# A one-layer hybrid encoder on one core: memory's loads and transposes moved ahead, a row factor put into the rotary tables

## The chip, the cores and the metric

One NeuronCore of a Trainium2 chip runs the whole layer as one program. The metric is device microseconds of an execution, the median of several runs. All data are float32. Each large product is made of three TensorE products of float32r parts (high times high, high times low, low times high), so a weight or an activation is first split into a rounded part and a rest.

## The reference

One layer, with 512 positions of 1024 features, and 256 memory rows of 1024 features:

```python
h = rmsnorm(x, pre_mix_g)
aq, ak, av, hq, hf_fwd, hf_bwd, hi, hg = split_columns(h @ w_in, IN_SPLITS)
aq = rmsnorm(aq per head, q_norm_g); ak = rmsnorm(ak per head, k_norm_g)
att = axial_gqa_attention(apply_rope(aq, cos, sin), apply_rope(ak, cos, sin), av)
rec = hgrn2_group(hq, hf_fwd, hf_bwd, hi, hg, lb, out_g)
x = x + rmsnorm(concatenate([att, rec]) @ w_out, post_mix_g)
h, m = rmsnorm(x, pre_x_g), rmsnorm(mem, mem_norm_g)
x = x + rmsnorm(memory_cross_attention(h, m, w_xq, w_xkv, w_xo), post_x_g)
h = rmsnorm(x, pre_ffn_g)
x = x + rmsnorm(conv_ffn(h, w_up, conv_w, conv_b, w_down), post_ffn_g)
```

Attention has 8 query heads of 64 on 2 key heads; the recurrent group (HGRN2) has 4 heads of 128 and runs in both directions.

## The kernel before

Weights arrive as 132 units of 128x1024, in the order of use. A unit is loaded on SP's queue (L117) and split: units 7 to 41 by a cast on ScalarE (`wh`, L127), a negation (`wl`, units 7 to 27 on ScalarE, L129; 28 to 41 on GpSimd, L131) and a DMA on GpSimd's queue that adds the weight to `wl` in flight (L132); the others by a cast (L104) and a subtraction on VectorE (L105). Three units are prepared ahead of the one in use. TensorE multiplies them at L150, L151 and L152.

Row 1/rms(x) is never multiplied into x: the projections use x times the gain, and each output row is scaled by `r` afterwards.

The mixing stage weaves two streams of program text. One, `mix_projections`, holds the projections: the output gate (`put_sg`), the three projections of heads 1, 2 and 3 (`hgrn_in`), the queries, and keys and values (`put_kv`). The other, `cores`, holds the recurrences of heads 0, 1 and 2 (`hgrn_core`). A recurrence goes level by level: a copy on ScalarE (L514), eight small products (L517, PSUM bank tag `ps_c`), multiplications and a predicated copy on VectorE (L543, L549); then L524, L529, L534, L555 to L557, the squares of its output (L561), the row factor on GpSimd (L168, L169) and a transpose (L571). A scheduling layer then fixes each engine's order of instructions by its own estimates, and each engine runs its list strictly in order; a wait holds all that is behind it on that engine. Loads that ScalarE or GpSimd issue stand in the same list as its arithmetic.

Memory's part of this stage: `mem_norm` asks for the norm's weight (L163) and memory's two blocks of 128 rows (L660) on GpSimd's queue, squares them on ScalarE (L203) and scales them on VectorE (L185). `mem_turn` transposes them on TensorE (L194) through the two PSUM banks `ps_b`, with a split to high and low parts after each (L104, L105). Their projections to keys begin when the mixing projections are over.

Queries and keys go through `norm_rope`: squares (L594), a sum per head (L596), the power -1/2 on GpSimd (L168, L169), a multiplication of that factor by `r` on GpSimd (L598), and on VectorE two products with the rotary tables (L603, L606), their sum (L607) and the product with the head's factor (L608). The tables, cosine and sine times the gains of the norms, are made once by `rope_tables` from a load on GpSimd's queue (L581). For keys a cast (L618) and a subtraction (L619) follow, and `turn_k` transposes the result into `kT` (L626, copied out by L627) through the same banks `ps_b` as the memory keys (`put_kx`) use at that time.

All pools are shared: 16 buffers `big`, and PSUM banks in pairs with the tags b, s, o and c.

Of the kernel before, what the change touches and what calls it, by code (L numbers as in the profile page):

```python
# [14 lines left out]
ALU = mybir.AluOpType  # L15
# [3 lines left out]
P = 128  # L19
D = 1024  # L20
T = 512
NB = T // P
KC = D // P
M = 256
MB = M // P
# [4 lines left out]
AHEAD = 3  # L30
HOLD_BLOCK = 4
TURN_STEP, MEM_TURN, UP_TURN = 0, (0, 4), (0, 2)
NEG_SCALAR = frozenset(range(7, 28))
NEG_POOL = frozenset(range(28, 42))
CORE_SHARE, ATT_LEAD = 53.0, 4.0
KEY_TURNS = {1: (0, 1), 2: (2, 3)}
WARM, SPREAD_STEP = 4, 2
# [37 lines left out]
def layer(tc, io, out):  # L75
    nc = tc.nc
# [14 lines left out]
    def bank(tag):  # L91
        return ps.tile([P, 512], F32, name="ps_" + tag, tag=tag)

    def big(shape, dt=F32):
        return b8.tile(shape, dt, name="big", tag="big")
# [7 lines left out]
    def split(hi, lo, src, eng=None):  # L103
        nc.scalar.copy(hi, src)  # L104
        (eng or nc.vector).tensor_sub(lo, src, hi.bitcast(F32))  # L105
# [15 lines left out]
    def issue():  # L121
# [3 lines left out]
        wl = wp.tile([P, 1024], F32R, name="wl", tag="wl")  # L125
        if i in NEG_SCALAR or i in NEG_POOL:
            nc.scalar.copy(wh, raw)  # L127
            if i in NEG_SCALAR:
                nc.scalar.mul(wl, wh.bitcast(F32), -1.0)  # L129
# [24 lines left out]
    def blk(b):  # L154
        return slice(b * P, (b + 1) * P)

    def rows_bc(src, n):
        return src[None, :].to_broadcast([P, n])

    def gains(*names, eng=None):  # L160
        g = big([P, 2, D])
        for i, name in enumerate(names):
            (eng or nc.gpsimd).dma_start(g[:, i, :], rows_bc(io[name], D))  # L163
        return [g[:, i, :] for i in range(len(names))]
# [7 lines left out]
    def half(c):  # L172
        return slice(c * 512, c * 512 + 512)
# [10 lines left out]
    def scale_rows(xb, r, g, h, c):  # L184
        nc.vector.scalar_tensor_tensor(out=h[:, half(c)], in0=xb[:, half(c)], scalar=r, in1=g[:, half(c)],  # L185
                                       op0=ALU.mult, op1=ALU.mult)

    def turn_in(h, act, b, tags, before=None):
        for c in range(2):
            if before:  # L190
                before(c)
            o = bank(tags[c]).rearrange("p (k n) -> p k n", k=4)
            for k in range(4):
                nc.tensor.transpose(o[:, k, :], h[:, blk(c * 4 + k)], ident)  # L194
            hi, lo = act.hi, act.lo
            if len(hi) == 2:
                split(hi[c][:, :, blk(b)], lo[c][:, :, blk(b)], o)
            else:
                split(hi[0][:, c * 4:c * 4 + 4, blk(b)], lo[0][:, c * 4:c * 4 + 4, blk(b)], o)
# [62 lines left out]
    def proj_tm(act, tags, use, n=512):  # L262
        o = [bank(t) for t in tags]
        nk = 1024 // n
        for j in range(8 // nk):
            w = unit(nk)
            for b in range(len(tags)):
                for k in range(nk):
                    kc = nk * j + k
                    mm3(o[b][:, :n], act.get(kc, blk(b)), (w[0][:, k, :], w[1][:, k, :]), kc == 0, kc == 7)  # L270
                if kc == 7:
                    use(b, o[b])
                yield 3 * nk * MM * n / 512
# [121 lines left out]
    r = rstd_of(rx[:, :NB], NB, D, rx[:, NB:])  # L395
# [48 lines left out]
    sg_box, heads, qkv, rec_done = [], {}, {}, [0]  # L444
# [20 lines left out]
    def hgrn_in(h, between=()):  # L465
        qk = big([P, 2, 2, T])
        tt = big([P, 2048])
        q = tmp2(tag="tq")

        def put_q(z):  # L470
            nc.scalar.activation(q, z, ACT.Sigmoid)
            nc.vector.tensor_mul(q, z, q)

        def put_f(d):
            def put(z):
                f = tt[:, d * T:(d + 1) * T]
                k = qk[:, 1, d, :]
                nc.scalar.activation(f, z, ACT.Sigmoid)
                nc.scalar.activation(k, z, ACT.Sigmoid, scale=-1.0)
                nc.scalar.activation(f, f, ACT.Identity, scale=oml[:, d, h:h + 1], bias=lb[:, d, h:h + 1])  # L480
                nc.vector.scalar_tensor_tensor(out=qk[:, 0, 1 - d, :], in0=f, scalar=oml[:, d, h:h + 1], in1=q,
                                               op0=ALU.mult, op1=ALU.mult)
            return put

        for put in (put_q, put_f(0), put_f(1)):
            yield from proj_fm(hT, T, "b", scaled(put))
            for job in between[:3]:
                job()
            between = between[3:]
        heads[h] = (q, qk, tt)  # L490
# [85 lines left out]
        yield 0.5  # L576

    def rope_tables():
        both = big([P, 6, NB, 64])
        rope, cs = both[:, 0:4], both[:, 4:6]  # L580
        nc.gpsimd.dma_start(cs, io["rope"])  # L581
        nc.vector.tensor_scalar(qkg[:, 0, :], qkg[:, 0, :], 0.125, None, op0=ALU.mult)
        for i in range(2):
            nc.vector.tensor_mul(rope[:, 2 * i], cs[:, 0], qkg[:, None, i, :].to_broadcast([P, NB, 64]))
            gs = pat(qkg, i * 64 + 1, [[0, NB], [2, 32], [-1, 2]])
            nc.vector.tensor_tensor(out=rope[:, 2 * i + 1].rearrange("p b (i two) -> p b i two", two=2),
                                    in0=cs[:, 1].rearrange("p b (i two) -> p b i two", two=2), in1=gs, op=ALU.mult)
        return rope

    def norm_rope(z, nh, which, b):  # L590
        n = nh * 64
        rope = qkv["rope"]
        u = tmp2()
        nc.scalar.activation(u[:, :n], z, ACT.Square, scale=r[:, b:b + 1])  # L594
        ss = small()
        nc.vector.tensor_reduce(ss[:, :nh], u[:, :n].rearrange("p (h d) -> p h d", h=nh), axis=AX.X, op=ALU.add)  # L596
        rz = rstd_of(ss[:, :nh], nh, 64)
        nc.gpsimd.tensor_scalar(rz[:, :nh], rz[:, :nh], r[:, b:b + 1], 0.0, op0=ALU.mult, op1=ALU.add)  # L598
        xn = tmp2()
        x3 = xn[:, :n].rearrange("p (h d) -> p h d", h=nh)  # L600
        st = rope[:, 2 * which + 1, b, :]
        ss4 = st.rearrange("p (i two) -> p i two", two=2)[:, None].to_broadcast([P, nh, 32, 2])
        nc.vector.tensor_tensor(out=u[:, :n].rearrange("p (h i two) -> p h i two", h=nh, two=2),  # L603
                                in0=pat(z, 1, [[64, nh], [2, 32], [-1, 2]]), in1=ss4, op=ALU.mult)
        ct = rope[:, 2 * which, b, :][:, None, :].to_broadcast([P, nh, 64])
        nc.vector.tensor_tensor(out=x3, in0=z.rearrange("p (h d) -> p h d", h=nh), in1=ct, op=ALU.mult)  # L606
        nc.vector.tensor_add(xn[:, :n], xn[:, :n], u[:, :n])  # L607
        nc.vector.tensor_tensor(out=x3, in0=x3, in1=rz[:, :nh, None].to_broadcast([P, nh, 64]), op=ALU.mult)  # L608
        return x3
# [12 lines left out]
    def turn_k(b):  # L622
# [3 lines left out]
            nc.tensor.transpose(o[:, i, :].bitcast(F32R), kd4[:, i, :], ident_r)  # L626
        nc.scalar.copy(qkv["kT"][:, :, blk(b)], o)  # L627

    def open_qkv():
        qkv["rope"] = rope_tables()  # L630
        qkv["kT"] = big([P, 4, T], F32R)
        qkv["vv"] = const.tile([P, NB, 2, 2, 64], F32R, name="vv")
        qkv["qT"] = [big([P, 4, T], F32R) for _ in range(2)]
# [18 lines left out]

    kv = {}

    def mem_norm():
        g_mem, = gains("mem_norm_g")
        kv["rows"] = big([P, MB, D])
        for b in range(MB):
            m = kv["rows"][:, b, :]
            nc.gpsimd.dma_start(m, io["mem"][blk(b), :])  # L660
            r = row_rstd(m, tmp4([P, D]))
            for c in range(2):
                scale_rows(m, r, g_mem, m, c)

    def mem_turn():
        kv["m"] = Act([big([P, 8, M], F32R)], [big([P, 8, M], F32R)])
        for b in range(MB):
            turn_in(kv["rows"][:, b, :], kv["m"], b, "bb")

    def mix_projections():  # L670
        yield from proj_tm(hT, tm_tags, put_sg)
        yield from hgrn_in(1)
        mem_norm()
        yield from hgrn_in(2)
        open_qkv()
        zs, roped = {}, {}
        yield from proj_tm(hT, tm_tags, zs.__setitem__)

        def rope_job(b):
            return lambda: roped.__setitem__(b, rope_q(b, zs[b]))  # L680

        def turn_job(b):
            return lambda: turn_q(b, roped[b])

        jobs = [rope_job(0), rope_job(1)]
        for b in range(NB):
            jobs.append(turn_job(b))
            if b + 2 < NB:
                jobs.append(rope_job(b + 2))
        mem_turn()  # L690
        yield from hgrn_in(3, jobs)
        yield from proj_tm(hT, tm_tags, put_kv, 256)

# [356 lines left out]
```

## Time and profile before

| what | value |
|---|---|
| median of 3 runs (lowest, highest) | 852.19 us (851.39, 852.71) |
| the profiled execution's own time | 850.9 us |
| its span, first to last instruction | 849.0 us |
| mean granted TensorE clock | 0.993 |
| TensorE busy | 831.3 us, 98% of the span |
| VectorE busy | 490.7 us, 58% |
| ScalarE busy | 426.4 us, 50% |
| GpSimd busy | 102.7 us, 12% |

In the rows of a timeline the first number is the start in microseconds from the beginning of the span and the second the duration; the bracket at the end gives how long the engine stood idle before the row and what ended that. A matmul's duration includes its way through the array, so consecutive rows overlap: the pace is the distance between starts. A row of several equal instructions carries their count.

### The profile page before, as it was taken

How to read it: one execution, taken by the hardware profiler on the slowest of the kernel's cores; microseconds unless marked ns; L12 is line 12 of the kernel's file. 1: busy time of each engine (PE TensorE's matmuls, PEld its weight loads, DVE VectorE, ACT ScalarE, POOL GpSimd, SP SyncE). 2: the span in 40 equal slices, each digit the busy share in tenths (PEclk: the TensorE clock that was granted, in tenths of full speed). 3: DMA queues.
4: the chain of work that ended last, by engine and by line, in shares of the span. 5: the costliest groups of instructions: out<-in, count | busy, mean ns of one | idle time of the engine just before them, and what ended most of it. 6: DMA issues, size and time to landing. Idle time of an engine off the chain costs nothing.

```text
span 849.0 us, 11082 instructions
## 1 busy us (share of the span) xinstructions
PE 831.3 (98%) x4304; PEld 705.0 (83%) x4304; DVE 490.7 (58%) x759; ACT 426.4 (50%) x736; POOL 102.7 (12%) x163
## 2 busy tenths in 40 slices
PE   9999999999899999999999999999999999999996
PEld 7888777889799888888888998888888888888885
DVE  5364487479786875854443865555555557722224
ACT  6675656467688874644543643333333335511121
POOL 0111211057223201300001300000000000000001
PEclk9999999999899999999999999999999999999999
DMA  8686854556667633252312243223332332222212
GB/s 313 189 200 136 223 126 96 107 142 146 157 143 167 138 117 132 75 174 75 101 48 75 76 135 97 95 94 100 100 100 99 100 100 81 100 95 96 100 49 100
DMA packets 29796, 101.81 MB, mean 120 GB/s; under 512 B 3952, under 2 KB 4464, under 8 KB 29744
## 3 DMA queue, kind: packets, MB, share of 16 engines
q1 hardware_dynamic: 22752, 77.38, 27.0%
q0 software_dynamic: 6272, 22.81, 14.4%
q10 hardware_dynamic: 720, 0.92, 0.3%
q8 instruction: 34, 0.56, 0.3%
q14 instruction: 18, 0.15, 0.1%
HBM read 99.00 MB, written 2.10 MB: 119 GB/s over the span
## 4 chain that ended last, share of the span: by engine, by line
PE 92%; ACT 2%; POOL 2%; DMA 1%; DVE 1%; issue 1%; POOLq 0%; DVEq 0%; ACTq 0%
PE ps_b L150 9%; PE ps_b L151 9%; PE ps_b L152 9%; PE ps_s L152 6%; PE ps_s L151 6%; PE ps_s L150 6%; PE ps_o L150 6%; PE ps_o L152 6%; PE ps_o L151 6%; PE ps_c L151 4%; PE ps_c L150 4%; PE ps_c L152 4%; PE ps_c L517 3%; PE ps_o L754 2%; PE ps_s L732 2%; PE ps_o L742 2%
## 5 line engine op out<-in xcount | busy, mean ns | idle before, releaser
L105 DVE TENSOR_TENSOR wl<-raw,wh 128x1024 fp32r<-128x1024 f32 x93 | 113.8, 1223 | 199.6 <-ACT wh L104 199.5
L104 ACT CAST wh<-raw 128x1024 fp32r<-128x1024 f32 x93 | 98.0, 1053 | 205.2 <-PE ps_o L152 71.4
L150 PE MATMUL ps_b<-big,wh 128*128 128x512 f32 (+1 forms) x320 | 119.5, 373 | 0.0
L152 PE MATMUL ps_b<-big,wl 128*128 128x512 f32 (+1 forms) x320 | 118.0, 369 | 0.0
L151 PE MATMUL ps_b<-big,wh 128*128 128x512 f32 (+1 forms) x320 | 117.9, 368 | 0.0
L152 PEld LDWEIGHTS ps_b<-big,wl 128*128 128x128 f32 x320 | 61.5, 192 | 9.4
L151 PEld LDWEIGHTS ps_b<-big,wh 128*128 128x128 f32 x320 | 61.6, 193 | 9.3
L150 PEld LDWEIGHTS ps_b<-big,wh 128*128 128x128 f32 x320 | 61.5, 192 | 9.2
L178 POOL TENSOR_SCALAR small<-small 128x1 f32<-128x1 f32 x40 | 13.9, 348 | 439.1 <-ACT tmp L209 420.2
L543 DVE TENSOR_TENSOR big<-big 128x512 f32<-128x512 f32 x64 | 47.3, 747 | 17.6 <-PE ps_c L517 12.7
L150 PE MATMUL ps_s<-wh,big 128*128 128x512 f32 (+1 forms) x140 | 53.7, 383 | 0.0
L151 PE MATMUL ps_s<-wl,big 128*128 128x512 f32 (+1 forms) x140 | 53.2, 380 | 0.0
L152 PE MATMUL ps_s<-wh,big 128*128 128x512 f32 (+1 forms) x140 | 53.2, 380 | 0.0
L127 ACT CAST wh<-raw 128x1024 fp32r<-128x1024 f32 x35 | 36.6, 1048 | 31.1 <-PE ps_b L151 17.5
L150 PE MATMUL ps_o<-wh,big 128*128 128x512 f32 (+1 forms) x124 | 47.8, 386 | 0.0
L151 PE MATMUL ps_o<-wl,big 128*128 128x512 f32 (+1 forms) x124 | 47.0, 379 | 0.0
L152 PE MATMUL ps_o<-wh,big 128*128 128x512 f32 (+1 forms) x124 | 46.8, 378 | 0.0
L132 POOL DMA_DIRECT2D wl<-in_w_dram x35 | 31.0, 886 | 115.8 <-ACT wl L129 104.2
L105 DVE TENSOR_TENSOR big<-ps_o,big 128x512 fp32r<-128x512 f32 x52 | 35.7, 687 | 13.4 <-ACT big L104 13.2
L104 ACT CAST big<-ps_o 128x512 fp32r<-128x512 f32 x52 | 30.5, 586 | 19.4 <-PE ps_o L857 7.5
L517 PE MATMUL ps_c<-big,tmp 128*128 128x128 f32 x224 | 33.4, 291 | 4.1 <-ACT tmp L514 3.2
L517 PEld LDWEIGHTS ps_c<-big,tmp 128*128 128x128 f32 x224 | 30.3, 194 | 8.4 <-ACT tmp L514 6.4
(246 smaller groups left out, 1961.0 us busy)
## 6 DMA issues: line engine op xcount, KB each, us to landing
raw<-in_w_dram SPq DMA_DIRECT2D x131, 512.0 KB, 3.3
wl<-in_w_dram POOLq DMA_DIRECT2D x35, 512.0 KB, 5.5
big<-in_x_dram SPq DMA_DIRECT2D x8, 512.0 KB, 6.2
big<-in_xt_dram SPq DMA_DIRECT2D x3, 512.0 KB, 8.5
big<-in_mem_dram POOLq DMA_DIRECT2D x2, 512.0 KB, 8.2
out_dram<-big SPq DMA_DIRECT2D x4, 256.0 KB, 2.0
out_dram<-big ACTq DMA_DIRECT2D x3, 256.0 KB, 2.0
big<-in_xt_dram SPq DMA_DIRECT2D x2, 256.0 KB, 3.5
```

The costliest lines, as they stand in the source:

```text
L104: nc.scalar.copy(hi, src)
L105: (eng or nc.vector).tensor_sub(lo, src, hi.bitcast(F32))
L127: nc.scalar.copy(wh, raw)
L132: nc.gpsimd.dma_start(wl, io["w"][i], accum_op=ALU.add)
L150: nc.tensor.matmul(o, a[0], b[0], start=start, stop=False)
L151: nc.tensor.matmul(o, a[0], b[1], start=False, stop=False)
L152: last_mm[0] = nc.tensor.matmul(o, a[1], b[0], start=False, stop=stop).ins
L517: nc.tensor.matmul(o[:, b, :], kc[:, blk(b)], pat(qk, b * P, [[2 * m, P // (2 * m)], [T + m, 2], [1, m]]), start=True, stop=True)
L543: nc.vector.tensor_tensor(out=c, in0=c, in1=pat(tt, toff + off, [[2, npair], [gap, 2], [0, m]]), op=ALU.mult)
L732: nc.tensor.matmul(s, qT[h // 4][:, h % 4, blk(qb)], kT[:, 2 * (h // 4) + c, :], start=c == 0, stop=c == 1)
L742: nc.tensor.transpose(o[:, c, :], e[:, 0, blk(c)], ident)
L754: nc.tensor.matmul(o, vv[:, c, h // 4].rearrange("p a d -> p (a d)"), pt[:, j, c, :], start=c + j == 0, stop=c == 3 and j == 1)
```

## The change

Four things are changed. The names in the diff are those of the section on the kernel; line numbers after the first part shift by up to nine in the new file.

- Memory's norm weight, its two row blocks (`mem_load`) and the rotary tables (`load_tables`) are asked for on ScalarE's queue, at the start of `mix_projections`. Before, they were asked for on GpSimd's queue where they are used.
- `r` is multiplied into cosine and sine, once per block of 128 positions, by four small ScalarE instructions (L581 of the new file); the multiplication on GpSimd in each `norm_rope` (L598) is gone, eight instructions in all.
- `mem_turn` stands between the projections of head 2 and the queries, no longer behind the queries, and its transposes use the banks `ps_s` and `ps_o`, which the projection of the queries takes right behind it.
- Units 28, 29 and 30 are negated on ScalarE (L129) and no longer on GpSimd (L131).

```diff
-NEG_SCALAR = frozenset(range(7, 28))
-NEG_POOL = frozenset(range(28, 42))
+NEG_SCALAR = frozenset(range(7, 31))
+NEG_POOL = frozenset(range(31, 42))
...
     def rope_tables():
-        both = big([P, 6, NB, 64])
-        rope, cs = both[:, 0:4], both[:, 4:6]
-        nc.gpsimd.dma_start(cs, io["rope"])
+        rope, cs = qkv["tables"][:, 0:4], qkv["tables"][:, 4:6]
+        for b in range(NB):
+            nc.scalar.mul(cs[:, :, b, :], cs[:, :, b, :], r[:, b:b + 1])
...
         rz = rstd_of(ss[:, :nh], nh, 64)
-        nc.gpsimd.tensor_scalar(rz[:, :nh], rz[:, :nh], r[:, b:b + 1], 0.0, op0=ALU.mult, op1=ALU.add)
...
+    def load_tables():
+        qkv["tables"] = big([P, 6, NB, 64])
+        nc.scalar.dma_start(qkv["tables"][:, 4:6], io["rope"])
...
-    def mem_norm():
-        g_mem, = gains("mem_norm_g")
+    def mem_load():
+        kv["g"], = gains("mem_norm_g", eng=nc.scalar)
         kv["rows"] = big([P, MB, D])
         for b in range(MB):
+            nc.scalar.dma_start(kv["rows"][:, b, :], io["mem"][blk(b), :])
+
+    def mem_norm():
+        for b in range(MB):
             m = kv["rows"][:, b, :]
-            nc.gpsimd.dma_start(m, io["mem"][blk(b), :])
...
-            turn_in(kv["rows"][:, b, :], kv["m"], b, "bb")
+            turn_in(kv["rows"][:, b, :], kv["m"], b, "so")
...
     def mix_projections():
+        mem_load()
+        load_tables()
         yield from proj_tm(hT, tm_tags, put_sg)
         yield from hgrn_in(1)
         mem_norm()
         yield from hgrn_in(2)
+        mem_turn()
         open_qkv()
...
-        mem_turn()
         yield from hgrn_in(3, jobs)
```

ScalarE's list in the first recurrence (head 0), before; `wh` and `wl` are parts of weight units, L478 to L480 the gates of head 0, L502, L508 and L514 belong to the recurrence:

```order
L127 CAST wh<-raw 128x1024 x2
L129 ACTIVATE wl<-wh 128x1024
L478 ACTIVATE big<-tmp_442 128x512
L479 ACTIVATE big<-tmp_442 128x512
L480 ACTIVATE big<-big,lb,oml 128x512
L129 ACTIVATE wl<-wh 128x1024
L502 ACTIVATE tmp_466<-big,oml 128x512
L514 COPY tmp_481<-big 128x512
L127 CAST wh<-raw 128x1024
```

And the same place now:

```order
L127 CAST wh<-raw 128x1024
L163 DMA big<-in_mem_norm_g_dram 128x1024
L129 ACTIVATE wl<-wh 128x1024
L478 ACTIVATE big<-tmp_442 128x512
L479 ACTIVATE big<-tmp_442 128x512
L480 ACTIVATE big<-big,lb,oml 128x512
L662 DMA big<-in_mem_dram 128x1024 x2
L630 DMA big<-in_rope_dram 128x512
L127 CAST wh<-raw 128x1024
L502 ACTIVATE tmp_473<-big,oml 128x512
L129 ACTIVATE wl<-wh 128x1024
L514 COPY tmp_488<-big 128x512
```

Four DMA issues have come in, and one cast and one negation of weights have changed places with the recurrence's first steps. In TensorE's list the first products of this recurrence (L507) now stand behind 20 more products of the gate's projection than before.

GpSimd's list where keys are normalised (`small` holds the heads' factors), before:

```order
L169 TENSOR_TENSOR small<-small,nhalf 128x2
L598 TENSOR_SCALAR small<-small,rx 128x2
L131 TENSOR_SCALAR wl<-wh 128x1024
L132 DMA wl<-in_w_dram 128x1024
L168 TENSOR_SCALAR small<-small 128x2
```

And now:

```order
L169 TENSOR_TENSOR small<-small,nhalf 128x2
L168 TENSOR_SCALAR small<-small 128x2
L169 TENSOR_TENSOR small<-small,nhalf 128x2
L132 DMA wl<-in_w_dram 128x1024
L168 TENSOR_SCALAR small<-small 128x2
```

The multiplication by `r` and the negation have gone from between the powers; the first L131 now stands behind the last key's power.

TensorE's list at the end of head 1's recurrence (L571 is its output's transpose, `ps_s` and `ps_o` the projection of the queries), before:

```order
L152 MATMUL ps_s<-wh,big 128x512
L150 MATMUL ps_o<-wh,big 128x512
L151 MATMUL ps_o<-wl,big 128x512
L571 MATMUL ps_c<-ident,tmp_1063 128x128
L152 MATMUL ps_o<-wh,big 128x512
L571 MATMUL ps_c<-ident,tmp_1063 128x128 x2
```

And now (L194 are memory's transposes):

```order
L150 MATMUL ps_b<-big,wh 128x512
L151 MATMUL ps_b<-big,wh 128x512
L152 MATMUL ps_b<-big,wl 128x512
L194 MATMUL ps_s<-ident,big 128x128 x4
L194 MATMUL ps_o<-ident,big 128x128 x4
L194 MATMUL ps_s<-ident,big 128x128 x4
L194 MATMUL ps_o<-ident,big 128x128 x4
L571 MATMUL ps_c<-ident,tmp_1065 128x128 x3
L150 MATMUL ps_s<-wh,big 128x512
```

Memory's 16 transposes have come here from behind the queries; they now stand ahead of L571, where before only products of the projections did.

More of the change, by code (lines that the diff above doesn't have):

```diff
@@ L653, in layer @@
     kv = {}
-    def mem_norm():
-        g_mem, = gains("mem_norm_g")
+    def mem_load():
+        kv["g"], = gains("mem_norm_g", eng=nc.scalar)
         kv["rows"] = big([P, MB, D])
         for b in range(MB):
+            nc.scalar.dma_start(kv["rows"][:, b, :], io["mem"][blk(b), :])
+    def mem_norm():
+        for b in range(MB):
             m = kv["rows"][:, b, :]
-            nc.gpsimd.dma_start(m, io["mem"][blk(b), :])
             r = row_rstd(m, tmp4([P, D]))
             for c in range(2):
-                scale_rows(m, r, g_mem, m, c)
+                scale_rows(m, r, kv["g"], m, c)
     def mem_turn():
```

## The prediction

> **What bounds the kernel.** The page comes first, and of it the row of busy times:
>
> ```profile
> PE 831.3 (98%) x4304; PEld 705.0 (83%) x4304; DVE 490.7 (58%) x759; ACT 426.4 (50%) x736; POOL 102.7 (12%) x163
> ```
>
> TensorE (PE) bounds the kernel and the change takes no product from it: only the stretches where it stands still, or runs at a lower clock, can be won. Busy times by stretch show where these lie:
>
> ```profile
> 100.00:115.00 15.00, 11.78 (x54) 9.60 (x53) 10.75 (x19) 8.50 (x13) 3.46 (x6) 0.89 0.80 190
> 130.00:145.00 15.00, 13.54 (x86) 11.43 (x85) 10.08 (x22) 9.92 (x22) 2.92 (x4) 1.00 0.41 104
> 205.00:227.00 22.00, 17.81 (x124) 17.03 (x123) 18.76 (x43) 12.36 (x24) 12.62 (x18) 0.84 0.77 183
> ```
>
> The first number after the stretch's length is PE's busy time, the third from the end the granted clock: 11.78 of 15, 13.54 of 15, 17.81 of 22, two of the three with the clock down. I read each in the timeline.
>
> Stall A, PE's and ScalarE's (ACT) rows, with memory's second block from the chain of waits:
>
> ```profile
> 103.97 0.39 PE L152 MATMUL ps_b<-big,wl 128*128 128x512 f32 x1
> 104.42 0.39 PE L151 MATMUL ps_b<-big,wh 128*128 128x512 f32 x1
> 108.03 1.59 PE L517 MATMUL ps_c<-big,tmp 128*128 128x128 f32 x8 [3.22 <-ACT tmp L514]
> 109.32 0.71 PE L152 MATMUL ps_b<-big,wl 128*128 128x512 f32 x1
> 113.35 1.12 PE L517 MATMUL ps_c<-big,tmp 128*128 128x128 f32 x8
> ...
> 105.62 1.06 ACT L203 ACTIVATE tmp<-big 128x1024 f32<-128x1024 f32 x1 [3.10 <-DMA big<-in_mem_dram]
> ...
> 96.89 8.65 DMA big<-in_mem_dram
> ```
>
> The block asked for at 96.89 took 8.65 us. ACT stood 3.10 us at its squares (L203), and the recurrence's copy L514, the releaser in the bracket at 108.03, was behind them in ACT's list.
>
> Stall B, PE's rows, then VectorE's (DVE) and GpSimd's (POOL):
>
> ```profile
> 210.91 0.28 PE L152 MATMUL ps_b<-big,wl 128*128 128x256 f32 x1
> 211.03 0.28 PE L150 MATMUL ps_b<-big,wh 128*128 128x256 f32 x1
> 211.39 1.20 PE L517 MATMUL ps_c<-big,tmp 128*128 128x128 f32 x8
> 212.97 0.54 PE L626 MATMUL ps_b<-ident_r,big 128*128 128x128 f32 x4 [0.39 <-DVE big L105]
> 216.75 0.75 PE L626 MATMUL ps_b<-ident_r,big 128*128 128x128 f32 x4 [3.24 <-DVE big L105]
> 222.23 0.61 PE L517 MATMUL ps_c<-big,tmp 128*128 128x128 f32 x4
> ...
> 205.33 0.29 DVE L608 TENSOR_TENSOR tmp<-tmp,small 128x128 f32<-128x128 f32 x1 [0.55 <-POOL small L598]
> 211.28 1.11 DVE L608 TENSOR_TENSOR tmp<-tmp,small 128x128 f32<-128x128 f32 x1
> 215.25 1.11 DVE L608 TENSOR_TENSOR tmp<-tmp,small 128x128 f32<-128x128 f32 x1 [0.17 <-POOL small L598]
> 216.29 0.41 DVE L105 TENSOR_TENSOR big<-ps_b,big 128x256 fp32r<-128x256 f32 x1
> ...
> 211.21 1.04 POOL L131 TENSOR_SCALAR wl<-wh 128x1024 fp32r<-128x1024 f32 x1
> 212.55 0.91 POOL L132 DMA_DIRECT2D wl<-in_w_dram  x1 [0.30 <-POOL wl L131]
> 215.19 1.04 POOL L131 TENSOR_SCALAR wl<-wh 128x1024 fp32r<-128x1024 f32 x1
> ```
>
> The key's transpose L626 needs the bank that DVE's L105 frees at 216.70, and L105 is queued behind L608, which waits for POOL's chain of powers, itself queued behind L131 and L132. Besides, L608 takes 1.11 us beside a L131 and 0.29 without one.
>
> Stall C, the transpose at the end of head 1:
>
> ```profile
> 136.27 0.39 PE L151 MATMUL ps_o<-wl,big 128*128 128x512 f32 x1
> 137.70 0.30 PE L571 MATMUL ps_c<-ident,tmp 128*128 128x128 f32 x1 [1.04 <-DVE tmp L567]
> 143.78 1.20 PE L517 MATMUL ps_c<-big,tmp 128*128 128x128 f32 x8 [0.41 <-DVE big L543]
> ```
>
> **What the stalls cost.** I compare the distance of starts with the pace of undisturbed rows. A 512-wide product comes every 0.225 us (103.97 to 104.42 holds two), a 256-wide one every 0.12 (210.91 to 211.03), and eight 128-wide ones take 0.89:
>
> ```profile
> 59.84 0.89 PE ps_c L517 x8
> ```
>
> A: 104.42 to 108.03 is 3.61 for one product, 3.4 lost. From 108.03 to 113.35 eight small and ten 512-wide products would take 0.89 + 2.25 = 3.14 and took 5.32, 2.2 lost to the lower clock. Together **5.6**.
> B: from 211.39 to 222.23 (10.84 us) there are 20 small products (2.2) and 18 256-wide ones (2.2): **6.4** lost.
> C: 136.27 to 137.70 less 0.23 is 1.2, and 0.4 at 143.78: **1.6**.
> Sum 13.6 us, the most that the change can win if all three go and nothing comes.
>
> **Part by part.** *Early loads.* Memory's rows are now asked for some 45 us before their squares, so stall A has no cause left. The two squares now stand behind head 0's L561 in ACT's list, where ACT stood idle (bracket):
>
> ```profile
> 86.34 1.05 ACT L127 CAST wh<-raw 128x1024 fp32r<-128x1024 f32 x1 [4.09 <-PE ps_b L151]
> 845.32 0.34 ACTq L958 DMA_DIRECT2D out_dram<-big  x1
> ```
>
> Two of 1.06 fit into 4.09: nothing. The four issues, at 0.34 each (second row), are 1.4 us ahead of L502 in ACT's list. Their cover is in TensorE's list: L507, which waits for L502's result, stands 20 products later, 4.5 us. I take nothing; without the cover it is 1.4. What the loads meet on the way is dearer:
>
> ```profile
> 45.00:62.00 17.00, 16.59 (x90) 13.75 (x89) 12.60 (x24) 11.43 (x16) 2.59 (x3) 1.00 0.96 218
> 62.00:70.00 8.00, 8.00 (x49) 7.06 (x48) 5.32 (x10) 3.15 (x4) 0.86 (x1) 1.00 0.57 131
> 315.00:320.00 5.00, 5.00 (x31) 4.30 (x31) 2.62 (x5) 3.60 (x8) 0.95 (x2) 1.00 1.00 382
> ...
> wl<-in_w_dram POOLq DMA_DIRECT2D x3, 512.0 KB, 8.0
> ```
>
> The next to last number is the share of the DMA engines: 0.96 from 45 to 62, where three weight accumulations (last row, the issues of 46 to 62) took 8.0 us each. Into this come 1.75 MB (norm weight 0.5, rows 1.0, tables 0.25), 4.6 us of all engines at 382 GB/s, so the backlog ends near 66.6 instead of 62. Who needs something first? The tables: ACT scales them right behind the fourth L514,
>
> ```profile
> 58.64 0.62 ACT L514 COPY tmp<-big 128x512 f32<-128x512 f32 x1 [1.52 <-DVE big L543]
> 201.76 0.36 ACT L594 ACTIVATE tmp<-ps_s,rx 128x128 f32<-128x128 f32 x1
> ```
>
> which was at 58.64 and, with the recurrence 4.5 later, ends near 63.8. The fifth L514 is wanted by 65.2. The scaling, four instructions of at most 0.36 (the nearest row, of the same 128x128), fits between the two only if the tables have landed. Landing times between 58 and 66.6 are open; the cost is 0 to 3.4 us. I take 1.2.
>
> *Tighter recurrences.* Heads 0 and 1 now have 4 or 5 products between most levels where before there were 4 to 13. A level with 4 in between costs 0.89 + 0.90 = 1.79 of PE, and these two starts, four products between them, lie 2.01 apart:
>
> ```profile
> 117.89 1.08 PE ps_c L517 x8
> 119.90 1.08 PE ps_c L517 x8
> ```
>
> So 0.2 per such level; 0 to 1.6 for some eight of them, I take 0.8.
>
> *Transposes ahead of L571.* Sixteen at 0.11 give 1.8 us more work ahead of it and cover stall C's 1.2. In return the queries' projection waits for banks that DVE must empty, four splits of the size of
>
> ```profile
> L105 DVE TENSOR_TENSOR big<-ps_o,big 128x512 fp32r<-128x512 f32 x52 | 35.7, 687 | 13.4 <-ACT big L104 13.2
> ```
>
> 2.7 us, mostly beside the 2 us of products and L507 that stand between. 0 to 2.7; I take 0.4, since the four banks are wanted one after the other.
>
> *The row factor and the negations.* L598 and, up to the last key, L131 leave POOL's list. The slow L608 lose 0.8 each, DVE's waits go, and L105 should come some 3 us earlier, about when PE asks. Three negations move to ACT:
>
> ```profile
> L129 ACT ACTIVATE wl<-wh 128x1024 fp32r<-128x1024 f32 x19 | 20.1, 1055 | 0.2
> ```
>
> 3.2 us in all; ACT has idle time for them (12.36 busy of 22), but one stands with a cast ahead of the last key's cast (2.1 us), and L105 of the second memory key is behind that in turn. A rest of 0 to 3 us, I take 0.8.
>
> Sum: 13.6 less 1.2, 0.8, 0.4 and 0.8 = 10.4 us. The profiled execution took 850.9 us (span 849.0), 1.3 below the median 852.19; 10.4 off gives 840.5 for it and **841.8** for a median.
>
> **The rivals.**
> *Tables land late.* The Trainium skill, "DMA: Bandwidth & Descriptors", section "Queues, rings and completion order", says that each DMA engine goes round the queues that have work, a packet at a time. By it ACT's queue would get a third beside SP's and POOL's and, holding as many bytes as POOL's, end with them. This rule speaks against the change; no row here has three queues loaded at once. As a mechanism of this kernel: the tables, last in ACT's queue, land with the end of the backlog at 66.6; with 1.4 of scaling and 0.62 of L514 PE waits from 65.2 to 68.6, 3.4, and then runs slow as in stall A, 2.2. With the other costs (2.0) that leaves 13.6 − 2.0 − 5.6 = 6.0: 846.2. For it speaks the share 0.96; against it that a queue with two loads waiting moves on faster.
> *Stall B stays.* DVE is busy 18.76 of 22 us there; if its backlog or ACT's 2.1 us hold L105 as long as POOL did, 6.4 is not won: 13.6 − 6.4 − 2.4 = 4.8, 847.4. Against it: L608's 0.8 each come back in any case.
> *Slower.* ACT's queue is served only when POOL's is empty. Three accumulations of 8.0 from 50 on end at 74, and the tables after them, say at 78. All of ACT's list waits behind the scaling, L514 and the weights' casts alike. PE then stands from 65.2 to 80.0, 14.8, and 2.2 slow: 13.6 − 2.0 − 17.0 = −5.4, 857.6. It turns from gain to loss when the tables land at 72.6. Against it: SP's loads got on beside POOL's.
> *No change.* The change doesn't do what it says, because ACT reaches the loads no earlier than needed, or the four costs come at their upper ends (3.4 + 1.6 + 2.7 + 3.0 = 10.7) with a slow stretch of 2.2 behind one of them: 0.7 is left, 851.5. ACT's list, where they stand ahead of L502, speaks against it.
>
> **The numbers.** Forecast 0.63, late tables 0.15, stall B stays 0.12, slower 0.06, no change 0.04. A difference under 0.2%, 1.7 us, can't be told from none. Faster: 0.63 + 0.15 + 0.12 = 0.90; same 0.04; slower 0.06. The range goes from 838.5 (13.6, no cost) to 848.0, past both smaller gains; outside are the last two cases and some of the tails.
>
> **What would show it.** Right: no ACT wait at L203, no PE wait over 1 us at L626 or L571, the clock at 1.00 from 100 to 230, the span near 838.6. Wrong: ACT waiting for the tables at L581 with PE at L517 behind it, near 64; PE waiting at L151 or L152 for a `wl` between 50 and 75; L626 still waiting for L105; PE waiting for L105 at the first products of the queries.

## The result and the profile after

The kernel after takes 840.75 us in the median (839.84 to 844.02, four runs), the kernel before, run beside it, 852.09 (851.39 to 852.71): ratio 0.9874, 95% interval 0.9845 to 0.9903. The forecast was 841.8. The profiled execution of after took 839.84 us; its span, 838.1, is 10.9 shorter than that of before. First the page's busy row, then the three stretches in the windows view, columns as before:

```profile
PE 826.9 (99%) x4304; PEld 700.8 (84%) x4304; DVE 488.0 (58%) x759; ACT 430.8 (51%) x743; POOL 91.8 (11%) x148
```

```profile
100.00:115.00 15.00, 14.82 (x88) 11.92 (x87) 14.31 (x27) 8.29 (x13) 1.72 (x2) 1.00 0.66 146
130.00:145.00 15.00, 14.60 (x79) 11.98 (x78) 13.17 (x25) 10.54 (x16) 1.79 (x2) 1.00 0.50 116
205.00:227.00 22.00, 20.14 (x153) 18.56 (x152) 18.41 (x36) 17.05 (x34) 4.85 (x6) 1.00 0.66 151
```

PE is busy for 14.82 us where it was for 11.78, 14.60 for 13.54 and 20.14 for 17.81, and the granted clock, 0.89 and 0.84 before in the first and the last, stays at 1.00. Stall A is gone, B is not quite. Its place in the timeline of after, engine by engine:

```profile
206.10 1.20 PE L517 MATMUL ps_c<-big,tmp 128*128 128x128 f32 x8 [0.38 <-DVE tmp L607]
207.51 0.54 PE L625 MATMUL ps_b<-ident_r,big 128*128 128x128 f32 x4 [0.22 <-ACT big L626]
208.81 0.39 PE L150 MATMUL ps_b<-big,wh 128*128 128x256 f32 x1 [0.76 <-DVE big L105]
214.62 0.53 PE L625 MATMUL ps_b<-ident_r,big 128*128 128x128 f32 x4 [0.51 <-ACT big L626]
...
205.81 0.27 DVE L607 TENSOR_TENSOR tmp<-tmp,small 128x128 f32<-128x128 f32 x1
206.62 1.47 DVE L543 TENSOR_TENSOR big<-big 128x512 f32<-128x512 f32 x1
208.35 0.41 DVE L105 TENSOR_TENSOR big<-ps_b,big 128x256 fp32r<-128x256 f32 x1
...
206.50 1.05 POOL L131 TENSOR_SCALAR wl<-wh 128x1024 fp32r<-128x1024 f32 x1
```

L607 (L608 before) takes 0.27 where it took 1.11, and the waits of 3.24 are four of 0.2 to 0.8. The L131 of unit 31, which stayed on GpSimd, now meets L543.

To place the gain I add up, over PE's timeline, what each distance of starts has beyond the pace (0.227, 0.120 and 0.110 us for products 512, 256 and 128 wide), in stretches cut at the same places of the program. The stretches' figures, in us, of the profiled executions:

| stretch | before | rows early alone | after | loads alone | POOL step back | negations back | both back | transposes back | tables first | unit 31 too |
|---|---|---|---|---|---|---|---|---|---|---|
| head 0 (from 50) | 2.0 | 3.2 | 2.1 | 10.9 | 2.9 | 3.9 | 3.3 | 3.0 | 2.1 | 2.6 |
| head 1, with A (from 100) | 6.6 | 2.1 | 2.3 | 1.8 | 2.2 | 2.2 | 2.1 | 2.2 | 2.2 | 2.1 |
| with C | 3.2 | 1.8 | 2.1 | 1.8 | 2.2 | 2.2 | 2.3 | 1.4 | 2.1 | 2.3 |
| with B | 7.8 | 7.3 | 3.1 | 7.2 | 4.8 | 6.1 | 6.5 | 4.7 | 3.1 | 1.9 |
| with B, less the halved clock | 5.4 | 5.8 | 3.1 | 5.7 | 3.4 | 4.6 | 5.0 | 3.2 | 3.1 | 1.9 |
| attention | 3.1 | 2.9 | 3.1 | 3.1 | 3.1 | 3.0 | 3.0 | 3.1 | 3.1 | 3.7 |

After against before: 4.2 in A, 1.1 in C, 4.7 in B, nothing lost in head 0; the other 0.9 of the span's 10.9 lie outside these stretches. The other columns are the experiments below.

Each column is one execution, and one thing in it moves by itself. In the traces the granted clock is either whole or one half, and behind some waits it stays at one half for 3.41 us or twice that. Products that run at one half lose 1.4 to 1.5 us in 3.41 us. In B's stretch this came twice in before (215.33 to 222.16, 2.4 us), once in six of the others and not at all in after, tables first and unit 31; the row below B's has it taken off. So of the 4.7 won in B 2.3 are waits and 2.4 are clock.

### The profile page after: what moved, and what is told of

It reads as the page before. It is cut to its first block, busy times and chain, and to the rows that moved or that the text cites. A ratio compares the mean times of both kernels' runs of the same rounds, so it can differ in the third digit from the quotient of the medians.

```text
span 838.1 us, 11074 instructions
## 1 busy us (share of the span) xinstructions
PE 826.9 (99%) x4304; PEld 700.8 (84%) x4304; DVE 488.0 (58%) x759; ACT 430.8 (51%) x743; POOL 91.8 (11%) x148
## 4 chain that ended last, share of the span: by engine, by line
PE 95%; DVE 2%; DMA 1%; ACT 1%; issue 0%; SPq 0%; POOL 0%; POOLq 0%; DVEq 0%
PE ps_b L150 10%; PE ps_b L152 10%; PE ps_b L151 10%; PE ps_s L152 6%; PE ps_s L151 6%; PE ps_s L150 6%; PE ps_o L150 6%; PE ps_o L152 6%; PE ps_o L151 6%; PE ps_c L150 4%; PE ps_c L152 4%; PE ps_c L151 4%; PE ps_c L517 3%; PE ps_o L762 2%; PE ps_s L740 2%; PE ps_o L750 2%
## 5 line engine op out<-in xcount | busy, mean ns | idle before, releaser
L105 DVE TENSOR_TENSOR wl<-raw,wh 128x1024 fp32r<-128x1024 f32 x93 | 113.8, 1224 | 199.6 <-ACT wh L104 199.4
L150 PE MATMUL ps_b<-big,wh 128*128 128x512 f32 (+1 forms) x320 | 118.2, 370 | 0.8 <-DVE big L105 0.8
L151 PE MATMUL ps_b<-big,wh 128*128 128x512 f32 (+1 forms) x320 | 116.5, 364 | 0.0
L150 PEld LDWEIGHTS ps_b<-big,wh 128*128 128x128 f32 x320 | 60.3, 189 | 9.7 <-DVE big L105 0.9
L151 PEld LDWEIGHTS ps_b<-big,wh 128*128 128x128 f32 x320 | 60.4, 189 | 9.1
L543 DVE TENSOR_TENSOR big<-big 128x512 f32<-128x512 f32 x64 | 48.4, 761 | 15.1 <-PE ps_c L517 8.8
L151 PE MATMUL ps_s<-wl,big 128*128 128x512 f32 (+1 forms) x140 | 53.0, 379 | 0.0
L151 PE MATMUL ps_o<-wl,big 128*128 128x512 f32 (+1 forms) x124 | 46.8, 377 | 0.0
L105 DVE TENSOR_TENSOR big<-ps_o,big 128x512 fp32r<-128x512 f32 x54 | 37.1, 688 | 13.4 <-ACT big L104 13.2
L132 POOL DMA_DIRECT2D wl<-in_w_dram x35 | 30.8, 881 | 119.5 <-ACT wl L129 104.5
L150 PE MATMUL ps_b<-wh,big 128*128 128x512 f32 x92 | 36.9, 401 | 0.0
L151 PE MATMUL ps_b<-wl,big 128*128 128x512 f32 x92 | 36.0, 392 | 0.0
```

What stands on the lines that cost most here:

```text
L132: nc.gpsimd.dma_start(wl, io["w"][i], accum_op=ALU.add)
L150: nc.tensor.matmul(o, a[0], b[0], start=start, stop=False)
L151: nc.tensor.matmul(o, a[0], b[1], start=False, stop=False)
L543: nc.vector.tensor_tensor(out=c, in0=c, in1=pat(tt, toff + off, [[2, npair], [gap, 2], [0, m]]), op=ALU.mult)
```

## Experiments

Each ratio is to the kernel before, run on the same chip beside it, whose median was 850.13 to 851.24 in these groups; ratios compare kernels of different groups, medians do not quite.

**The loads alone**

```diff
 (before)
+        mem_load()
+        load_tables()
         yield from proj_tm(hT, tm_tags, put_sg)
```

> The kernel before with the early loads alone: memory's norm weight, its rows and the tables are asked for on ScalarE's queue at the start of the mixing stage; the row factor stays in L598, the negations stay, the transposes stay. My theory is that each part takes away its own stall and that the loads cost nothing on the way. Then stall A goes and B and C stay: 4.2 to 5.6 us less than the kernel before, 846.5 to 848.0, with PE still waiting some 3 us for L105 at L626 and 1 us for L567 at L571. A rival: the stalls hang together, since an earlier end of the recurrences shifts what meets in B. Then this kernel wins clearly more or less than that, for instance over 8 us or under 2.

Measured 853.57 us, ratio 1.0034 (1.0023 to 1.0046): slower than before. Neither theory had that; the rival's "under 2" covers the number, but for another reason. VectorE's and PE's rows:

```profile
63.97 0.42 DVE L582 TENSOR_TENSOR big<-big,qkg 128x256 f32<-128x256 f32 x1 [11.93 <-DMA big<-in_rope_dram]
64.98 1.10 DVE L543 TENSOR_TENSOR big<-big 128x512 f32<-128x512 f32 x1
67.53 2.05 PE L517 MATMUL ps_c<-big,tmp 128*128 128x128 f32 x8 [6.71 <-DVE big L543]
```

The scheduling layer, which takes a load asked for early to be there early, put the products with the tables (L582, L584) ahead of head 0's L543 in VectorE's list. The tables landed at 63.9, VectorE stood 11.93 us and PE 6.71. It is the forecast's rival of the late tables, on another engine. In the kernel after the four L581 on ScalarE stand ahead of these products, and both come later in the lists.

**Memory's rows early, and nothing else**

```diff
 (before)
+        mem_load()
         yield from proj_tm(hT, tm_tags, put_sg)
```

> The kernel before with memory's norm weight and rows asked for early on ScalarE's queue, and nothing else: the tables are loaded and used where they were, near the end of head 1. My theory is that the early loads alone gained 2 us less than nothing because the products with the tables had come to stand in VectorE's list in the middle of head 0, ahead of the tables' landing. Then this kernel has no such wait: stalls A and C go, B stays, 4 to 6 us less than the kernel before, ratio 0.993 to 0.995. The rival is that the crowd of loads itself costs what A gave: 0.999 to 1.004.

Measured 844.99 us, 0.9932 (0.9915 to 0.9950), about 5.8 us. The windows of this kernel, and PE's wait that is left:

```profile
100.00:115.00 15.00, 14.81 (x84) 11.82 (x82) 13.46 (x25) 9.57 (x14) 1.72 (x2) 1.00 0.73 162
130.00:145.00 15.00, 14.83 (x84) 12.41 (x83) 13.26 (x26) 9.84 (x14) 1.80 (x2) 1.00 0.59 128
205.00:227.00 22.00, 17.65 (x126) 16.54 (x125) 17.65 (x38) 12.78 (x25) 8.49 (x11) 0.92 0.76 168
```

```profile
PE ps_b L626 <- DVE big L105: 3.6, 2, 3.2
```

A and C have gone, B stands as it was. My theory holds: the crowd of loads does not cost what A gave.

**Stall B: one cause or two.** A multiplication by one in the place of L598, the negations of three units back on GpSimd, and both:

```diff
 (after)
+        nc.gpsimd.tensor_scalar(rz[:, :nh], rz[:, :nh], 1.0, 0.0, op0=ALU.mult, op1=ALU.add)
...
-NEG_SCALAR = frozenset(range(7, 31))
-NEG_POOL = frozenset(range(31, 42))
+NEG_SCALAR = frozenset(range(7, 28))
+NEG_POOL = frozenset(range(28, 42))
```

> The kernel after, with one small GpSimd multiplication (by one) put back behind each power in the normalisation of queries and keys, in the place of L598; the orders of PE, DVE and ScalarE are otherwise the same. My theory is that stall B came from L598 and L168/L169 standing behind the negations L131 on GpSimd, and that L598 by itself adds only its 0.5 us to the chain of each key: 0 to 1 us slower than after, 840.5 to 842. A rival: the additional step in the chain is what held the last keys. Then this kernel gets back most of B's 4.6, 844 to 846.

> The kernel after, with units 28, 29 and 30 negated on GpSimd again (L131). My theory is that the negations are the main cause of stall B: the powers stand behind L131 (1.04) and L132 (0.91) on GpSimd's list and L607 takes 1.1 instead of 0.3 beside each L131. Then 3 to 4.6 us of B come back: 843.5 to 845.5, with PE waiting over 1 us for L105 or ScalarE at the transposes of keys, L625. The rival that L598 was the cause gives under 1 us, 840.5 to 841.8.

> The kernel after with both put back, the small GpSimd multiplication behind each power and the negations of units 28 to 30 on GpSimd, so that GpSimd's list at the keys is that of before. If the two parts of the change add up, this costs the sum of the two kernels with one each; my theory expects all of what stall B gave, 4.0 to 5.0 us more than after, 844.8 to 845.8. A rival, that B went because the loads, the transposes or the recurrences ahead of it moved, expects it to stay near 841.

Measured: the step back 843.06 us, 0.9912 (0.9891 to 0.9934); the negations back 843.62, 0.9915 (0.9894 to 0.9936); both 845.16, 0.9937 (0.9917 to 0.9957). Both together bring most of B back, 3.4 of 4.7 us in its stretch and 4.4 in the median (5.4 by the ratios), so B went through these two parts. By the stretch as it stands they do not add up, 4.8, 6.1 and 6.5 us against 3.1, and the step's time was over what I expected and under its rival's. But each of the three has one halving of the clock there (from 212.25, 212.42 and 211.65). Without it the step costs 0.3 us in B's stretch, the negations 1.5 and both 1.9, which adds up; before, the waits there cost 2.3 more than after's. With the negations back, PE, VectorE and GpSimd stand thus:

```profile
211.28 0.54 PE L625 MATMUL ps_b<-ident_r,big 128*128 128x128 f32 x4 [2.90 <-DVE big L105]
...
206.07 1.07 DVE L607 TENSOR_TENSOR tmp<-tmp,small 128x128 f32<-128x128 f32 x1
209.76 1.13 DVE L607 TENSOR_TENSOR tmp<-tmp,small 128x128 f32<-128x128 f32 x1
...
205.19 1.82 POOL L131 TENSOR_SCALAR wl<-wh 128x1024 fp32r<-128x1024 f32 x1
209.26 1.49 POOL L131 TENSOR_SCALAR wl<-wh 128x1024 fp32r<-128x1024 f32 x1
```

Each L607 runs until the L131 beside it ends (207.14 and 207.01, 210.89 and 210.75), and L105 comes behind it: the mechanism of the forecast. With the step alone VectorE waits 0.49 us for L598, PE 1.11 for L608 instead of 0.38 for L607; the rest in that stretch is the lower clock (0.84 from 205 to 216). That need not be the step's doing: with the transposes back, where GpSimd's work is that of after, the clock fell there too. So the negations' part in B is shown; of the step little is, and what else made its median 2.3 us longer than after's is open.

**Transposes back to their old place**

```diff
 (after)
-        mem_turn()
         open_qkv()
...
+        mem_turn()
         yield from hgrn_in(3, jobs)
...
-            turn_in(kv["rows"][:, b, :], kv["m"], b, "so")
+            turn_in(kv["rows"][:, b, :], kv["m"], b, "bb")
```

> The kernel after with memory's transposes at their old place, behind the queries, and through the two banks ps_b again. My theory is that the moved transposes take away stall C by standing ahead of L571, and cost 0.7 in waits of the queries for the banks: 1.1 us slower than after or so, 841.3 to 842.5, with PE waiting some 1 us for L567 at L571. A rival: C went because the recurrence of head 1 ends at another place now, and the transposes bring nothing or cost: 840.0 to 841.0 and no wait at L571.

Measured 840.70 us, 0.9880 (0.9863 to 0.9897): no difference from after. Windows of this kernel:

```profile
130.00:145.00 15.00, 15.00 (x86) 12.71 (x85) 12.90 (x24) 9.45 (x14) 1.80 (x2) 1.00 0.64 142
205.00:216.00 11.00, 9.24 (x64) 8.59 (x62) 8.64 (x16) 6.42 (x13) 3.46 (x4) 0.84 0.88 200
```

PE is busy for all of the 15 us in which C had stood. My theory falls, the rival holds: the transposes were not what removed C. Before, the last L557 and the transpose L571 behind it were 3.5 us apart; here they are 4.1,

```profile
125.81 0.39 PE L557 MATMUL ps_c<-big 128*128 128x128 f32 x2
129.93 0.60 PE L571 MATMUL ps_c<-ident,tmp 128*128 128x128 f32 x4
```

because the schedule with memory's rows early put 4.1 us of products there (with the rows alone it is 4.1 too, 126.72 to 130.84). That is enough for the chain of L561, L168, L169 and L567.

**Tables first, and more bytes ahead of them**

```diff
 (after)
-        mem_load()
-        load_tables()
+        load_tables()
+        mem_load()
```

> The kernel after with the tables asked for first on ScalarE's queue, ahead of memory's norm weight and rows; all the orders of the engines are otherwise the same. The tables should land near 48 to 52 instead of 63. My theory is that after's profiled run escaped a wait for the tables by only 0.24 us, and that other runs of it pay up to 3 us there: the median falls by 0 to 1 us to 839.8 to 840.8, and the spread of the runs gets smaller (after: 839.8 to 844.0). A rival: the spread comes from the weights' accumulations, three of which run beside the loads and for which PE waited 0.6 to 1.7 us near 52 in three of four kernels with the early loads. Then nothing changes, 840.8 to 842, and that wait stays.

Measured 840.11 us (839.80 to 841.78), 0.9877 (0.9861 to 0.9894). The tables landed in 3.9 us instead of 15.2, and the time is that of after. In after they had been in time by a hair, as ScalarE's rows with the median time to landing show:

```profile
62.64 0.62 ACT L514 COPY tmp<-big 128x512 f32<-128x512 f32 x1 [0.55 <-DVE big L543]
63.16 1.28 ACT L581 ACTIVATE big<-big,rx 128x128 f32<-128x128 f32 x4
65.18 0.62 ACT L514 COPY tmp<-big 128x512 f32<-128x512 f32 x1 [0.74 <-PE ps_c L517]
```

```profile
big<-in_mem_dram ACTq DMA_DIRECT2D x2, 512.0 KB, 11.9
big<-in_rope_dram ACTq DMA_DIRECT2D x1, 256.0 KB, 15.2
```

Asked for at 47.76, they were there at 62.9, L581 began at 63.16, and 0.74 us of ScalarE's time was left before the next L514. That four runs of tables first spread less (2.0 us against 4.2) is too little to show more.

> The kernel after with the suspected cost doubled: memory's two row blocks are loaded once more, to a buffer that nobody reads, ahead of the tables on ScalarE's queue (1 MB more). The last two loads of that queue of 512 KB each landed 5 us apart, so by a third share the tables land up to 10 us later, near 73; by the rate of 382 GB/s of all engines only 2.7 us later, near 65.6. My theory of the rival with late tables is that ScalarE then waits at L581 and PE at L517 behind it, from 65: 3 to 10 us slower than after, 844 to 851, most likely 848. If the tables are not the last thing that decides, under 1 us.

Measured 841.44 us, 0.9894 (0.9876 to 0.9912); a miss. The added loads were put at 23.6 and 30.8 us, as their buffers were free by then, and doubled nothing where it was meant. The second attempt tied them behind memory's rows:

```diff
 (after)
         mem_load()
+        with tc.issue_after(kv["last"]):
+            for b in range(MB):
+                kv["last"] = nc.scalar.dma_start(tmp4([P, D]), io["mem"][blk(b), :]).ins
-        load_tables()
+        with tc.issue_after(kv["last"]):
+            load_tables()
```

> The kernel after with 1 MB more (memory's rows once more, to a buffer that nobody reads) on ScalarE's queue between memory's rows and the tables; the earlier attempt had these loads issued near 24 and 31, where they delayed nothing. In the orders the scaling L581 moves back a little, one of the four behind the fourth L514, three more later. By the rate of all engines the tables land 2.7 us later, near 66 to 67, by a third share for ScalarE's queue near 73. ScalarE waits for them from 64.9 with L514 behind it, and PE at L517 from 65.2 on: 1 to 8 us slower than after, with a clock below 1 behind it if the wait is over 3 us, 842 to 849.

Measured 843.57 us, 0.9912 (0.9896 to 0.9928), 3 us more than after. But not through the tables: they landed 17.2 us after their issue, at 66.4, 3.5 later than in after, near the 2.7 by the rate of all engines; and the schedule had moved L581 to 69.14, so nobody waited for them. PE lost its time at two other places of this kernel, by the list of its waits:

```profile
PE ps_s L151 <- DMA wl<-in_w_dram: 1.2, 1, 1.2
PE ps_c L571 <- DVE tmp L567: 0.8, 1, 0.8
```

So the price of late tables on ScalarE stays untried; the one measured is VectorE's 6.71 above.

**Memory's rows only behind the gate's projection**

```diff
 (after)
-        mem_load()
         load_tables()
         yield from proj_tm(hT, tm_tags, put_sg)
+        mem_load()
```

> The kernel after with only the tables asked for at the start of the mixing stage; memory's norm weight and rows are asked for behind the gate's projection, near 70 to 75, some 8 us ahead of their squares. My theory is that the crowd on the DMA engines from 45 to 63 is what the early loads cost: the wait of PE for a weight at 52 goes (0.6 to 1.7 us in three runs), the tables land near 52. If the rows land by 84, 839.5 to 840.5; a rival is that they land too late and ScalarE stands at L203 again with the gates of head 1 behind it: 842 to 846.

Measured 841.18 us, 0.9888 (0.9872 to 0.9905): no gain over after. PE's wait for a weight near 52 is gone and head 0's stretch is 1.6, the lowest of all, and ScalarE does not stand at L203 (82.71). So the crowd costs PE what that wait shows, by the distance of starts: nothing in the profiled runs of after, of tables first and of the spread keys, 0.4 to 1.7 in the nine others with early loads. That is no more than the runs of one kernel spread.

**What is left of B**

```diff
 (tables first)
-KEY_TURNS = {1: (0, 1), 2: (2, 3)}
+KEY_TURNS = {1: (0,), 2: (1, 2), 3: (3,)}
```

> The kernel with the tables asked for first, and in addition the transposes of the keys spread out: one key behind the second projection of memory's keys, two behind the third, one behind the fourth, where there were two and two behind the second and third. My theory is that what stays of stall B (three waits of 0.4 to 0.9 near 207 to 209 and one of 0.7 near 215) comes from two transposes in a row that wait for ScalarE's copies and for the two banks of the projections. Spread, 1 to 2 us of it go, and the lower clock behind them that some runs show with it: 838.0 to 839.5. A rival: attention starts later and finds less work beside it, so that the time stays or grows, 840 to 843.

Measured 841.63 us, 0.9892 (0.9874 to 0.9909): the rival. PE's waits of this kernel:

```profile
PE ps_o L750 <- DVE big L105: 1.0, 1, 1.0
PE ps_c L517 <- ACT tmp L514: 0.9, 1, 0.9
```

B's stretch lost nothing (3.1), its waits have changed places, and attention got a wait of 1.0.

```diff
 (tables first)
-NEG_SCALAR = frozenset(range(7, 31))
-NEG_POOL = frozenset(range(31, 42))
+NEG_SCALAR = frozenset(range(7, 32))
+NEG_POOL = frozenset(range(32, 42))
```

> The kernel with the tables asked for first, and one more negation, that of unit 31, on ScalarE. The negation leaves GpSimd at 206.5, where VectorE's L543 (1.47 instead of the 1.1 of the other one of its shape) runs beside it and L105, for which PE waits 0.9 at 208.8, stands behind; on ScalarE it comes behind the copy of the first key (L626) and ahead of that of the second. My theory, that what stays of B is VectorE and ScalarE having a little too much to do there, gives 0.3 to 0.8 us less than without it, 839.3 to 839.9, if PE's waits of 0.9 and 0.7 get shorter. A rival: the 1.05 on ScalarE delays the second key's copy and the recurrence's copy L514 behind it, and takes the place of what VectorE won: 840.0 to 842.

Measured 839.79 us (839.37 to 840.38), 0.9874 (0.9857 to 0.9890), against 0.9877 with the tables first alone and 0.9874 of after. PE's and VectorE's rows:

```profile
208.68 0.54 PE L625 MATMUL ps_b<-ident_r,big 128*128 128x128 f32 x4 [0.22 <-ACT big L626]
215.10 0.38 PE L150 MATMUL ps_b<-big,wh 128*128 128x256 f32 x1 [0.24 <-ACT big L626]
...
207.78 0.66 DVE L543 TENSOR_TENSOR big<-big 128x512 f32<-128x512 f32 x1
208.70 0.41 DVE L105 TENSOR_TENSOR big<-ps_b,big 128x256 fp32r<-128x256 f32 x1
```

The wait of 0.76 for L105 is gone, since L543 takes 0.66 without an L131 beside it where it took 1.47, and the last wait is 0.24 for 0.51: B's stretch falls from 3.1 to 1.9. Attention's takes half of that back (3.7 for 3.1), and in the ratio no gain can be told.

## Why the prediction was right, and where it was not

The three stalls were the right ones, each wait read rightly, and the sum of 10.4 came out at 10.7 (by the ratio; 11.3 by the medians). Its terms did not: the errors cancelled. A with its tighter recurrences gave 4.2 for 4.8, C 1.1 for 1.2, B 4.7 for 5.6, and the 1.2 set aside for late tables were not paid. That the total fits so well is luck; that it is near is not, since the causes of A and B held.

- **Stall A, 5.6.** Its cause is shown by the kernel with the rows early alone. The stretch gave 4.2: the recurrence of head 1, closer together now, keeps 0.2 us per level in it (as the forecast had for heads 0 and 1), and a wait of 0.3 at L517.
- **Early loads, 1.2.** This term stood for PE waiting behind the tables at L581, and it did not come: ScalarE waited at most 0.2 us for them in the kernels that scale them there, and PE not at all. What came instead, in nine other profiled runs and not in that of after, is a wait that the sum had no term for and the list of signs against it had, PE at L151 for a `wl`, 0.4 to 1.7 us. That it is of the same size is luck. The squares L203 ran without a wait, as said.
- **Late tables, rival.** The tables landed at 62.9, not with the backlog's end at 66.6. That end itself was near: the DMA engines' share is 0.93 from 63 to 66 and 0.59 from 66 to 70. But ACT's queue did not end with it. The forecast had three accumulations beside the loads, as before had them (issued at 47.64, 50.34 and 53.86); in after they were issued at 46.44, 51.28 and 59.24, the third after 7.10 us of waiting for ScalarE's `wl`, and that one landed behind the tables, at 66.3. The Trainium skill, "DMA: Bandwidth & Descriptors", section "Queues, rings and completion order", has each engine take the queues in turn, a packet at a time. The trace agrees as far as it goes: with three queues loaded, an accumulation issued at 46.44 took 10.2 us in after and memory's first block, of the same 512 KB and issued at 46.70, 9.8. The margin was narrow, though, and the loads alone show what missing it costs.
- **Tighter recurrences, 0.8.** In head 0 the stretch stayed at 2.0 to 2.1, in head 1 the levels cost what A's stretch keeps. Right in size, the place half wrong.
- **Transposes ahead of L571, 1.2 gained and 0.4 lost.** This step failed. C went with the schedule that the early rows brought, and without the moved transposes it stays away. The moved transposes gain nothing and cost 0.7 in that stretch (2.1 against 1.4), the waits of the queries' projection for its bank that stood on the list of signs; the forecast had 0.4.
- **Stall B, 6.4 less a rest of 0.8.** The mechanism is shown by putting GpSimd's work back, for the negations above all; the part of L598 is small. The rest was mis-sized: the stretch kept 3.1, of it four waits that sum to 2.5 by the distances of starts. The forecast looked for the rest at ScalarE's two instructions ahead of the last key's cast. PE's two waits for ScalarE there, at its copies L626, are 0.2 and 0.5; what the forecast had not seen is that the L131 that stays meets L543 and makes it 0.8 longer, ahead of L105.
- **Stall B staying, the slower case, no change.** None came. No transpose of keys waits for VectorE any more, and the tables were 10 us ahead of the turning point of 72.6. The other signs came out as listed: no wait at L203, no wait of PE over 1 us at L625 or L571, the clock at 1.00, the span at 838.1 for 838.6.

## What to carry to other kernels

A load that is asked for early moves its users early as well, where a scheduler sets the orders: look in the lists for what now stands behind the first user, since the load may land later than the scheduler believes. Where two causes feed one wait, put each back alone and both together, and take the time at a lower clock off before adding up: here two causes seemed to cost 1.7 and 3.0 us and both together 3.4, and by their waits they cost 0.3, 1.5 and 1.9. And undo each part by itself: of this change one part did nothing, and the stall that it was made to answer for had gone with another.

## What the hardware showed beyond that

- **VectorE beside GpSimd.** In six of six meetings of L608 (L607 after) with a negation (two each of before, of the negations back and of both back) this small VectorE product, 0.27 to 0.29 us alone, ended within 0.15 us of the end of the negation beside it; and with the negations back the negation grew too, to 1.82 and 1.49 from 1.04. Not every VectorE operation is held up: in before an L105 at 224.86, which reads a PSUM bank, took its usual 0.42 inside a negation (224.65 to 225.69).
- **The clock behind short waits.** In the kernel with the transposes back PE's waits near 206 to 209 are the same as after's within 0.03 us, and yet its granted clock is 0.84 from 205 to 216 where after's is 1.00. Start to start, three products took 0.64 us (209.47 to 210.11) where after has 0.36 (209.27 to 209.63), for 3.4 us, which made B's stretch 1.5 us longer:

```profile
209.47 0.41 PE L150 MATMUL ps_b<-big,wh 128*128 128x256 f32 x1
209.68 0.41 PE L151 MATMUL ps_b<-big,wh 128*128 128x256 f32 x1
209.89 0.41 PE L152 MATMUL ps_b<-big,wl 128*128 128x256 f32 x1
210.11 0.41 PE L150 MATMUL ps_b<-big,wh 128*128 128x256 f32 x1
```

```profile
209.27 0.28 PE L150 MATMUL ps_b<-big,wh 128*128 128x256 f32 x1
209.39 0.28 PE L151 MATMUL ps_b<-big,wh 128*128 128x256 f32 x1
209.51 0.28 PE L152 MATMUL ps_b<-big,wl 128*128 128x256 f32 x1
209.63 0.28 PE L150 MATMUL ps_b<-big,wh 128*128 128x256 f32 x1
```

What decides between the two shows when the trace is cut into stretches of 3.413 us, the unit in which the clock changes (in before it falls at 109.52 and 215.33, 31 such steps apart). Here the clock falls at 208.96, and the stretch before it holds all three waits; in after, whose clock falls only at 834.29, the stretch 184 steps before that holds two of them. First the two stretches of the kernel with the transposes back, then after's:

```profile
205.55:208.96 3.41, 2.07 (x15) 1.61 (x15) 3.41 (x7) 2.76 (x6) 2.78 (x3) 1.00 0.81 204
208.96:212.37 3.41, 3.41 (x17) 3.41 (x18) 2.35 (x5) 1.28 (x3) 0.00 (x0) 0.50 1.02 241
```

```profile
206.24:209.65 3.41, 2.44 (x19) 2.09 (x20) 3.41 (x6) 2.32 (x6) 2.08 (x3) 1.00 0.88 201
```

Six profiled kernels have these three waits. In two of them, this one and the first attempt at more bytes ahead, one stretch holds all three, 1.3 us in which PE stands, and the clock falls behind it; in the other four it holds 1.0 and the clock stays. The limit is not sharp by this measure: 1.32 us in one stretch with the rows early alone and 1.43 with the negations back had no fall behind them. The Trainium skill, "TensorE: Matmul & The Clock Gate", section "The HAM clock gate", says that the clock is set by how busy TensorE was in windows of about 3.4 us that run freely, whenever the kernel began. The traces agree, with steps of 3.41 us that begin at another place in each run. It may be part of why runs of one kernel spread by 2 to 4 us.
